# A gated-linear-attention block on one Trainium2 core: part of the operands made ahead is stored unsplit and split after loading

## The chip, the core and the metric

The kernel runs on one core of a Trainium2 chip. The core has five engines with a queue each: TensorE (PE; its weight loads are listed as PEld), VectorE (DVE), ScalarE (ACT), GpSimd (POOL) and SyncE (SP), which in this kernel issues the DMA transfers. Each engine takes its own instructions in order; between engines they wait on semaphores. The metric is the device time of one execution in microseconds, and the time of a kernel is the median of its runs.

## What is computed

One decoder block over 2048 positions of width 1024: a normalised input goes through one combined input projection into two mixers, a gated linear attention with 4 heads and a short gated convolution; their outputs go through an output projection and a residual add, then a feed-forward part with a residual add and a last normalisation.

```python
h = rmsnorm(x, norm1_g[l])
proj = h @ w_in[l]
p_q, p_k, p_v, p_g, p_a, c_b, c_c, c_h = jnp.split(proj, splits, axis=-1)
...
log_a = (jax.nn.log_sigmoid(gate_logits) / GATE_NORMALIZER)...
o = gla_chunked(q, k, v, log_a)
o = rmsnorm(o, gla_norm_g[l]) * jax.nn.silu(p_g)
u = c_c * c_h
o_conv = c_b * causal_depthwise_conv(u, conv_w[l])
mixed = jnp.concatenate([o_gla, o_conv], axis=-1) @ w_out[l]
x = x + mixed
h2 = rmsnorm(x, norm2_g[l])
ffn = (jax.nn.silu(h2 @ w_ffn_gate[l]) * (h2 @ w_ffn_up[l])) @ w_ffn_down[l]
x = x + ffn
```

Everything is float32.

## The kernel before

**Products of halves.** Activations are held transposed, features on the 128 partitions and positions along the free dimension, 512 positions to a tile. The 2048 positions are worked in two halves of 1024 (two tiles of 512, j = 0 and 1). A matrix product of one half with two blocks of 128 columns is a "unit": a two-by-two block product, done as in Strassen-Winograd with seven products instead of eight (`PRODUCTS`, line 35). The weight side of the seven is A11, S1, S2, A12, S3, S4, A22, and the input side is B11, T1, T2, B21, T3, B22, T4. The T's are differences of input blocks, the S's sums and differences of weight blocks that POOL makes (lines 342 to 349).

**Split operands.** A float32 operand is used as a pair: a rounded high part, made by ACT as a copy to `float32r`, and the rest, made by DVE as a subtraction (`split`, line 145, whose two instructions are lines 146 and 147). A product step is three matmuls of 128x128 weights with 128x512 inputs: high by high, high by rest, rest by high (`product_step`, lines 359 to 361). One product of a unit is four such steps over k. So each input operand is a buffer `op` of shape [128, 2, 512], and 28 of them (seven kinds, four k) serve all units of a half. The pool `opp` has just 28 such buffers. A unit's weights are split as it goes (`weight_quarter`, tile `wq`, four buffers).

**The first half** is built from loads (`build_first`). During its twelve input-projection units (`in_proj(0)`), background work is run in small steps, one for every second product (`tick`): the gates, row statistics, then `h1_ahead`, then the recurrence of the first half (`gla_half`).

**The second half's operands** are made ahead by `h1_ahead` (line 509). `combine` (line 222) loads the eight raw tiles of each half column, scales them on DVE (line 483), lets POOL make the differences (lines 247 to 260), and hands each of the 28 results to `put`, for each k in the order B11, T1, T2, T3, B21, T4, B22. `put` splits it into two scratch tiles, `hi` and `lo`, and stores both into DRAM (`s_h1`, seen in the trace as `siB` and `siT`). The scratch tiles come from a pool of 11 (`bx`), shared with everything else that the background does.

When the first half's units are all issued, `load_pairs(s_h1)` (line 519) loads the 28 pairs into `op` buffers, 512 KB each, in the order of `PRODUCTS`: B11, T1, T2, B21, T3, B22, T4. Each load waits until the buffer that it takes has had its last reader in the first half's last unit. All loads and stores go through the queue of SP (lines 138 and 141). Then come the second half's gates and its twelve units (`in_proj(1)`).

**Order.** The program text gives the dependences; the order of instructions on each engine is fixed when the kernel is built, by the tile framework's scheduler, and `issue_after` pins a few by hand. On the chip each engine follows that order.

Of the kernel before, what the change touches and what calls it, by code (L numbers as in the profile page):

```python
# [10 lines left out]
F32 = mybir.dt.float32  # L11
F32R = mybir.dt.float32r
# [6 lines left out]
P = 128  # L19
D = 1024  # L20
SEQ = 2048
PB = 512
# [12 lines left out]
PRODUCTS = [  # L35
    ("A11", "B11"), ("S1", "T1"), ("S2", "T2"), ("A12", "B21"),
    ("S3", "T3"), ("S4", "B22"), ("A22", "T4"),
]


LATER = ("B21", "T3", "B22", "T4")


C_G1, C_G2, C_GF, C_BG, C_GN, C_CW = 0, 8, 16, 24, 26, 27
# [4 lines left out]
def tile_hymba_block(ctx, tc, x, xt, win, wa, wgu, wout, wffn, wdown, wdown_first, small, out):  # L49
# [3 lines left out]
    def pool_of(name, bufs, **kw):  # L53
        return ctx.enter_context(tc.tile_pool(name=name, bufs=bufs, **kw))

    const = pool_of("const", 1)
    opp = pool_of("opp", 28)
# [5 lines left out]
    dram = pool_of("dram", 1, space=DRAM)  # L63
# [34 lines left out]
    def scratch(name, n):  # L98
# [17 lines left out]
    ]  # L116
    s_h2 = {n: [dram.tile([P, PB], F32, name=f"sf{n}_{k}") for k in range(4)] for n in LATER}
    s_h2p = {
        n: [dram.tile([P, 2, PB], F32, name=f"sh{n}_{k}") for k in range(4)] for _, n in PRODUCTS
    }  # L120
    s_h1 = {
        n: [dram.tile([P, 2, PB], F32, name=f"si{n}_{k}") for k in range(4)] for _, n in PRODUCTS
    }

    def col(c):
# [11 lines left out]
    def load(dst, src):  # L137
        return nc.sync.dma_start(dst, src)

    def store(dst, src):  # L140
        return nc.sync.dma_start(dst, src)
# [3 lines left out]
    def split(src, hi, lo):  # L145
        last_hi[:] = [act.activation(hi, src, AF.Copy)]  # L146
        return dve.tensor_tensor(lo, src, hi.bitcast(F32), ALU.subtract)  # L147
# [71 lines left out]
    def no_operands():  # L219
        return {b: [] for _, b in PRODUCTS}  # L220

    def combine(src, g, rb, put):


        order = [kj for k in range(4) for kj in ((k, 0), (k, 1), (k + 4, 1), (k + 4, 0))]
        ahead = deque()

        def fetch():
            if order:
                k, j = order.pop(0)  # L230
                h = bt("h")
                load(h[:], src(k, j))
                ahead.append((k, j, h))

        def quad():
            k, j, h = ahead.popleft()
            fetch()
            return scaled(col(g + k), rb[j], h)

        fetch()  # L240
        fetch()
        for k in range(4):
            b11 = quad()
            put("B11", k, b11)
            yield
            b12, t1 = quad(), bt("t1")
            pool.tensor_tensor(t1[:], b12[:], b11[:], ALU.subtract)
            put("T1", k, t1)
            yield
            b22 = quad()  # L250
            pool.tensor_tensor(t1[:], b22[:], t1[:], ALU.subtract)
            put("T2", k, t1)
            yield
            pool.tensor_tensor(b12[:], b22[:], b12[:], ALU.subtract)
            put("T3", k, b12)
            yield
            b21 = quad()
            put("B21", k, b21)
            yield
            pool.tensor_tensor(t1[:], b21[:], t1[:], ALU.subtract)  # L260
            put("T4", k, t1)
            yield
            put("B22", k, b22)
            yield
# [236 lines left out]
    def build_h():  # L501


        def quad(k, j):
            return scaled(col(C_G1 + k), rbs[j], raws[j, k])

        return build_first(quad, first_weights)

    def h1_ahead():

        def put(n, k, h):
            hi, lo = [bx[0].tile([P, PB], F32R, name=e, tag="b") for e in ("hi", "lo")]
            split(h[:], hi[:], lo[:])
            for e, y in enumerate((hi, lo)):
                store(s_h1[n][k][:, e, :], y[:].bitcast(F32))

        yield from combine(lambda k, j: xt[2 + j, :, k, :], C_G1, (rbs[2], rbs[3]), put)

    def load_pairs(src):
        ops = no_operands()  # L520
        for _, n in PRODUCTS:
            ops[n] = [load_pair(p) for p in src[n]]
        return ops

    def load_pair(src):
        o = opp.tile([P, 2, PB], F32R, name="op", tag="op")
        load(o[:].bitcast(F32), src[:])
        return o
# [279 lines left out]
    def h2_first(ssq, ops):  # L808
# [10 lines left out]
        def put(n, k, h):  # L819
            if n in LATER:  # L820
                store(s_h2[n][k][:], h[:])
            else:
                ops[n].append(split_op(h[:]))
# [3 lines left out]
    def h2_rest(ops):  # L827
        hs = deque()
        order = [(n, k) for n in LATER for k in range(4)]

# [205 lines left out]
    ops, first, differences = build_h()  # L1036
# [7 lines left out]
    in_proj(0, ops, first, differences)  # L1044
    drain_background(lambda: len(background) < 2)
    ops = load_pairs(s_h1)
    background.append(gate(1, ops))
    in_proj(1, ops)
# [120 lines left out]
```

## Time and profile before

| | |
|---|---|
| median of 3 runs | 2122.82 us (2122.73 to 2124.79) |
| profiled execution, its own time | 2120.33 us |
| its span | 2118.6 us |
| mean granted clock of TensorE | 0.989 |
| HBM read and written | 300.63 MB and 168.30 MB |
| stores of `hi` and `lo` by `h1_ahead` | 56 of 256 KB, issued from 140.6 to 229.6 us |
| loads of the 28 pairs | 28 of 512 KB, issued from 275.9 to 314.4 us |
| the second half's gate product (line 541) | up to 474 us |

In the profile, a line of the timeline has the start in us, the duration, the engine, the source line, the operation, the tiles written and read, and how often; in brackets behind it stands the engine's idle time just before and what ended it. An instruction made by a helper carries the helper's line: all splits are lines 146 and 147 and are told apart by their tiles (`hi`, `lo`, `wq`, `op`). "DMA to landing" is the time from the issue of a transfer on SP to its completion. Ends of matmuls are modelled, and their pitch, 0.23 us here, is shorter than their listed duration of 0.39.

### The profile page before, as it was taken

To read this page: it belongs to the slowest core of one execution; us is meant where nothing else is said; L and a number is where in the kernel's file an instruction comes from. 1 tells how busy PE (TensorE), PEld (TensorE's weight loads), DVE (VectorE), ACT (ScalarE), POOL (GpSimd) and SP (SyncE) were. 2 spreads that over 40 slices of the span, in tenths; PEclk is the share of its full clock that TensorE was granted. 3 is DMA by queue.
4 is the path that set the end of the run, shared out by engine and by line. 5 is a ranking of instruction groups with operands and counts; after the bars stand their busy time and mean duration, and the time that the engine had idled before them with its cause. 6 is when DMAs were issued, how large, how long until landed. Compare 5 with 4: busy or idle time off the path is not lost.

```text
span 2118.6 us, 26920 instructions
## 1 busy us (share of the span) xinstructions
PE 2038.3 (96%) x9133; PEld 1651.9 (78%) x9133; DVE 1412.8 (67%) x1983; ACT 1014.8 (48%) x1997; POOL 973.8 (46%) x703
## 2 busy tenths in 40 slices
PE   6999999999999999999999999999999989999996
PEld 4777787887888887778888878787888878877774
DVE  7668775548754696887887565555776766665554
ACT  5555444656543345544545453333554554543344
POOL 3435322222102364555564348764635544436774
PEclk9999999999999999999999999999999999999998
DMA  7349586433586882655655687697455535587662
GB/s 277 125 150 317 184 328 225 137 110 123 181 310 211 335 286 91 232 220 185 232 190 204 229 331 269 236 340 312 150 206 185 200 138 189 181 345 279 268 268 110
DMA packets 190971, 470.74 MB, mean 222 GB/s; under 512 B 20016, under 2 KB 65264, under 8 KB 181232
## 3 DMA queue, kind: packets, MB, share of 16 engines
q1 hardware_dynamic: 190832, 469.01, 60.8%
q8 instruction: 72, 1.18, 0.2%
q14 instruction: 67, 0.55, 0.1%
HBM read 300.63 MB, written 168.30 MB: 221 GB/s over the span
## 4 chain that ended last, share of the span: by engine, by line
PE 78%; DVE 8%; DMA 6%; issue 3%; ACT 2%; POOL 2%; SPq 0%; DVEq 0%; ACTq 0%; POOLq 0%
PE mm L359 22%; PE mm L361 22%; PE mm L360 22%; PE mm L777 2%; PE mm L778 2%; PE mm L780 2%; DVE wq L147 2%; DVE so L147 1%; DMA op<-shT 1%; DMA raw<-in_wffn_dram 1%; DMA raw<-in_wdown_dram 1%; PE a_ps L541 1%; DVE op L147 1%; ACT wq L146 1%; DMA raw<-in_win_dram 1%
## 5 line engine op out<-in xcount | busy, mean ns | idle before, releaser
L359 PE MATMUL mm<-op,wq 128*128 128x512 f32 x2499 | 983.0, 395 | 27.0 <-ACT c L379 10.7
L361 PE MATMUL mm<-op,wq 128*128 128x512 f32 x2499 | 968.3, 393 | 15.2 <-DVE wq L147 14.2
L360 PE MATMUL mm<-op,wq 128*128 128x512 f32 x2499 | 977.6, 391 | 0.0
L147 DVE TENSOR_TENSOR wq<-raw,wq 128x512 fp32r<-128x512 f32 (+2 forms) x626 | 523.3, 843 | 338.6 <-ACT wq L146 336.3
L146 ACT ACTIVATE wq<-raw 128x512 fp32r<-128x512 f32 (+2 forms) x626 | 363.9, 587 | 563.1 <-PE mm L361 407.0
L359 PEld LDWEIGHTS mm<-op,wq 128*128 128x128 f32 x2499 | 471.7, 189 | 141.8 <-ACT c L379 14.8
L361 PEld LDWEIGHTS mm<-op,wq 128*128 128x128 f32 x2499 | 471.5, 189 | 127.9 <-DVE wq L147 29.0
L360 PEld LDWEIGHTS mm<-op,wq 128*128 128x128 f32 x2499 | 472.0, 189 | 97.2 <-issue 1.0
L344 POOL TENSOR_TENSOR raw<-s,raw 128x512 f32<-128x512 f32 (+2 forms) x97 | 128.3, 1323 | 441.7 <-DVE wq L147 421.6
L383 DVE TENSOR_TENSOR c<-mm,c 128x512 f32<-128x512 f32 x267 | 182.9, 685 | 98.4 <-PE mm L361 94.7
L342 POOL TENSOR_TENSOR s<-raw 128x512 f32<-128x512 f32 (+2 forms) x97 | 130.0, 1340 | 206.7 <-DMA raw<-in_wffn_dram 84.8
L349 POOL TENSOR_TENSOR raw<-raw 128x512 f32<-128x512 f32 (+2 forms) x97 | 125.1, 1290 | 139.6 <-DVE wq L147 132.4
L379 ACT ACTIVATE c<-mm 128x512 f32<-128x512 f32 x267 | 154.7, 585 | 39.8 <-PE mm L361 37.4
L759 POOL TENSOR_TENSOR ssx<-ssx,q 128x512 f32<-128x512 f32 x52 | 76.1, 1476 | 155.4 <-ACT q L758 155.2
L343 POOL TENSOR_TENSOR raw<-raw 128x512 f32<-128x512 f32 (+2 forms) x97 | 137.4, 1416 | 4.1
L948 POOL TENSOR_TENSOR y<-c,y 128x512 f32<-128x512 f32 x66 | 98.7, 1498 | 49.0 <-DVE c L383 48.7
L147 DVE TENSOR_TENSOR so<-t,so 128x512 fp32r<-128x512 f32 x100 | 91.0, 916 | 23.6 <-ACT so L146 23.0
L146 ACT ACTIVATE wq<-s 128x512 fp32r<-128x512 f32 (+2 forms) x97 | 56.8, 586 | 95.4 <-PE mm L361 88.6
L777 PE MATMUL mm<-op,wq 128*128 128x512 f32 x256 | 100.9, 395 | 0.0
L778 PE MATMUL mm<-op,wq 128*128 128x512 f32 x256 | 99.8, 390 | 0.0
L147 DVE TENSOR_TENSOR wq<-s,wq 128x512 fp32r<-128x512 f32 (+2 forms) x97 | 85.0, 876 | 15.7 <-ACT wq L146 15.1
L146 ACT ACTIVATE so<-t 128x512 fp32r<-128x512 f32 x100 | 62.3, 626 | 39.2 <-DMA sa_B<-so 14.6
(175 smaller groups left out, 1884.4 us busy)
## 6 DMA issues: line engine op xcount, KB each, us to landing
raw<-in_wffn_dram SPq DMA_DIRECT2D x44, 1024.0 KB, 5.5
sa_T<-so SPq DMA_DIRECT2D x88, 512.0 KB, 5.0
op<-sa_T SPq DMA_DIRECT2D x88, 512.0 KB, 8.7
sa_B<-so SPq DMA_DIRECT2D x69, 512.0 KB, 3.4
op<-sa_B SPq DMA_DIRECT2D x69, 512.0 KB, 9.1
raw<-in_win_dram SPq DMA_DIRECT2D x23, 1024.0 KB, 5.3
raw<-in_wdown_dram SPq DMA_DIRECT2D x24, 768.0 KB, 6.2
sx<-y SPq DMA_DIRECT2D x48, 256.0 KB, 3.2
```

Of the source, the lines that this page charges most:

```text
L146: last_hi[:] = [act.activation(hi, src, AF.Copy)]
L147: return dve.tensor_tensor(lo, src, hi.bitcast(F32), ALU.subtract)
L342: pool.tensor_tensor(s1, a21, a22, ALU.add)
L343: pool.tensor_tensor(a21, a11, a21, ALU.subtract)
L344: pool.tensor_tensor(a11, s1, a11, ALU.subtract)
L359: pe.matmul(o[:], wh, xh, start=first and k == 0, stop=False, skip_group_check=True)
L360: pe.matmul(o[:], wh, xl, start=False, stop=False, skip_group_check=True)
L361: return pe.matmul(o[:], wl, xh, start=False, stop=k == n - 1, skip_group_check=True)
L379: act.activation(t[:], o[:], AF.Copy)
L383: dve.tensor_tensor(t[:], o[:], t[:], ALU.add)
L777: pe.matmul(o[e, j][:], wh, m[:, 0, :], start=k == 0, stop=False)
L778: pe.matmul(o[e, j][:], wh, m[:, 1, :], start=False, stop=False)
```

## The change

The three input kinds used last in a unit, T3, B22 and T4, are handled in another way; the other four (B11, T1, T2, B21) stay as they were.

- Their twelve DRAM tiles have one plane instead of two.
- In `h1_ahead`, `put` stores the unsplit tile and returns: no `hi`, no `lo`, one store of 256 KB.
- `load_whole` takes an `op` buffer, loads the unsplit tile into its second plane (256 KB), and splits it there: ACT writes the rounded part into the first plane, DVE subtracts and writes the rest over the loaded values.

```diff
+WHOLE = ("T3", "B22", "T4")
...
+    def made_ahead(name, n):
+        return dram.tile([P, PB] if n in WHOLE else [P, 2, PB], F32, name=name)
+
     s_h1 = {
-        n: [dram.tile([P, 2, PB], F32, name=f"si{n}_{k}") for k in range(4)] for _, n in PRODUCTS
+        n: [made_ahead(f"si{n}_{k}", n) for k in range(4)] for _, n in PRODUCTS
     }
...
         def put(n, k, h):
+            if n in WHOLE:
+                store(s_h1[n][k][:], h[:])
+                return
             hi, lo = [bx[0].tile([P, PB], F32R, name=e, tag="b") for e in ("hi", "lo")]
             split(h[:], hi[:], lo[:])
...
-            ops[n] = [load_pair(p) for p in src[n]]
+            ops[n] = [(load_whole if n in WHOLE else load_pair)(p) for p in src[n]]
         return ops
+
+    def load_whole(src):
+
+        o = opp.tile([P, 2, PB], F32R, name="op", tag="op")
+        load(o[:, 1, :].bitcast(F32), src[:])
+        split(o[:, 1, :].bitcast(F32), o[:, 0, :], o[:, 1, :])
+        return o
```

## The prediction

> **What bounds the kernel now.** I read the page first, then a table by stretches around the two places that the change touches, then the idle times of PE there.
>
> ```profile
> span 2118.6 us, 26920 instructions
> PE 2038.3 (96%) x9133; PEld 1651.9 (78%) x9133; DVE 1412.8 (67%) x1983; ACT 1014.8 (48%) x1997; POOL 973.8 (46%) x703
> PE 78%; DVE 8%; DMA 6%; issue 3%; ACT 2%; POOL 2%; SPq 0%; DVEq 0%; ACTq 0%; POOLq 0%
> ```
>
> PE is busy 96% of the span and holds 78% of the chain that ended last. So a few vector operations more or less count only where PE stands idle for them. The whole idle time of PE is 2118.6 - 2038.3 = 80 us, and only the part near the change can be won.
>
> The table by stretches has, behind the stretch and its length, busy us (instructions) of PE, PEld, DVE, ACT and POOL, then the granted clock, the DMA share and GB/s.
>
> ```profile
> 140.00:230.00 90.00, 82.71 (x349) 65.72 (x348) 81.89 (x103) 51.57 (x95) 51.00 (x32) 0.98 0.79 276
> 230.00:276.00 46.00, 43.71 (x184) 34.99 (x183) 31.07 (x45) 17.78 (x36) 15.28 (x10) 0.96 0.50 159
> 276.00:300.00 24.00, 24.00 (x115) 19.62 (x114) 18.53 (x27) 10.78 (x22) 5.90 (x5) 1.00 0.97 374
> 300.00:315.00 15.00, 15.00 (x83) 11.86 (x82) 9.10 (x19) 8.67 (x25) 2.92 (x3) 1.00 1.03 410
> 315.00:340.00 25.00, 23.31 (x115) 18.88 (x113) 12.96 (x23) 10.51 (x28) 6.76 (x5) 1.00 0.81 283
> ```
>
> From 140 to 230 us the second half's operands are made ahead, between the matmuls of the first half. There DVE is busy 91% and PE loses 7.3 us; PE loses 2.3 us more up to 276. From 276 to 315 the 28 operand pairs are loaded: the DMA engines are full (374 to 410 GB/s), PE has no idle time at all, and DVE has 11.4 us free of 39, ACT 19.6. So the two ends of the change lie in opposite stretches: it takes work from one where DVE decides and puts it into one where PE decides.
>
> PE's own idle times between 140 and 250 us, with their releasers, from the order of time:
>
> ```profile
> 150.49 0.50 PE L361 MATMUL mm<-op,wq 128*128 128x512 f32 x1 [2.08 <-DVE wq L147]
> ...
> 180.75 0.50 PE L359 MATMUL mm<-op,wq 128*128 128x512 f32 x1 [1.59 <-ACT c L379]
> ...
> 204.16 0.50 PE L361 MATMUL mm<-op,wq 128*128 128x512 f32 x1 [0.90 <-DVE wq L147]
> ...
> 220.00 0.50 PE L361 MATMUL mm<-op,wq 128*128 128x512 f32 x1 [1.75 <-DVE wq L147]
> ...
> 222.90 0.50 PE L359 MATMUL mm<-op,wq 128*128 128x512 f32 x1 [0.30 <-ACT c L379]
> ...
> 226.99 0.50 PE L361 MATMUL mm<-op,wq 128*128 128x512 f32 x1 [0.61 <-DVE wq L147]
> ...
> 246.09 0.50 PE L359 MATMUL mm<-op,wq 128*128 128x512 f32 x1 [2.08 <-ACT c L379]
> ```
>
> Every one waits for DVE's half of a weight split or for ACT's copy out of a bank: both stand in the same queues as the operand splits. After the first and the last the clock falls:
>
> ```profile
> 150.00:160.00 10.00, 9.51 (x35) 7.66 (x36) 10.00 (x11) 8.55 (x15) 7.31 (x5) 0.83 0.55 203
> 240.00:250.00 10.00, 7.81 (x28) 5.67 (x28) 7.94 (x13) 4.70 (x10) 1.85 (x2) 0.87 0.69 211
> ```
>
> A granted clock of 0.87 over 10 us costs at most 1.3 us more behind the stall at 246.
>
> **What is removed.** Of 28 splits made ahead, 12 go (T3, B22 and T4, four each): 12 ACT copies and 12 DVE subtractions. Of 56 stores of 256 KB, 12 go, and 24 of the scratch buffers are no longer taken. Their kinds in the trace (min/median/max ns):
>
> ```profile
> L146 ACT ACTIVATE hi<-h x16: 613/626/640, 140.0 to 226.5; 128x512 fp32r<-128x512 f32 x16
> L147 DVE TENSOR_TENSOR lo<-h,hi x16: 679/686/1781, 145.7 to 228.7; 128x512 fp32r<-128x512 f32 x16
> L147 DVE TENSOR_TENSOR c<-c,hi x16: 677/682/1779, 233.1 to 601.3; 128x512 fp32r<-128x512 f32 x16
> L147 DVE TENSOR_TENSOR lo<-t,hi x12: 676/688/1393, 151.0 to 226.9; 128x512 fp32r<-128x512 f32 x12
> ```
>
> The order per k is B11, T1, T2, T3, B21, T4, B22; counted off along DVE's subtractions, the removed ones of the last two k that stand in DVE's long backlog are these (single ones, with their neighbours):
>
> ```profile
> 204.02 0.68 DVE L147 TENSOR_TENSOR lo<-t,hi 128x512 fp32r<-128x512 f32 x1
> 204.62 0.68 DVE L147 TENSOR_TENSOR wq<-raw,wq 128x512 fp32r<-128x512 f32 x1
> 205.22 0.69 DVE L147 TENSOR_TENSOR lo<-h,hi 128x512 fp32r<-128x512 f32 x1
> ...
> 220.47 1.78 DVE L147 TENSOR_TENSOR lo<-h,hi 128x512 fp32r<-128x512 f32 x1
> ...
> 226.86 0.68 DVE L147 TENSOR_TENSOR lo<-t,hi 128x512 fp32r<-128x512 f32 x1
> ...
> 228.72 0.68 DVE L147 TENSOR_TENSOR lo<-h,hi 128x512 fp32r<-128x512 f32 x1
> ...
> 248.76 0.42 DVE L666 TENSOR_TENSOR kq<-kq,ee 128x256 f32<-128x256 f32 x1 [1.87 <-ACT ee L664]
> ```
>
> DVE stands in one unbroken queue from about 203 us to the idle time that ends at 248.76. In such a queue an instruction costs its pitch: 0.68 long, 0.60 from one start to the next (204.02, 204.62, 205.22), so 0.08 less than its length. The five removed ones cost 0.60 x 4 + 1.70 = 4.1 us. The idle times of PE in that stretch are 0.90 + 1.75 + 0.30 + 0.61 + 2.08 = 5.6 us, so 4.1 fits under them; of the clock's 1.3 us I take 1.0, as the idle time at 246, the last in the queue, should shrink most. **Gain here 5.1 us**, bounds 2 (the backlog is filled by waits for loads instead) and 5.6 + 1.3 = 6.9.
>
> The other seven removed subtractions lie between 158 and 200 us, where one idle time of PE stands, at 180.75. The ACT instruction ahead of that bank copy had waited for a scratch buffer:
>
> ```profile
> 178.58 0.63 ACT L146 ACTIVATE hi<-h 128x512 fp32r<-128x512 f32 x1 [1.51 <-DMA siT<-hi]
> ```
>
> With two buffers less per removed kind that wait should go: **gain 1.0 us** of 1.59, bounds 0 and 1.6. The stall at 150.49 lies ahead of the first removed split and stays.
>
> The 1.78 us of one subtraction against a median of 0.686 is a row to dwell on: it is in a stretch where POOL is busy 51 of 90 us. The Trainium skill (SBUF — State Buffer, Who interferes with whom) says that a DVE instruction with two SBUF inputs and a GpSimd instruction that reads SBUF hold one read interface in turn, the second waiting until the first is through. By that rule, the trace agrees, and each split moved to 276 to 315 us, where POOL is busy 8.8 us of 39, is cheaper there than it was.
>
> **What is added.** 12 ACT copies and 12 DVE subtractions behind the loads of T3, B22 and T4, and loads of 256 KB in place of 512 KB. Writing in place has its price in the trace: c<-c,hi takes 682 ns, as much as into another buffer (686). At the pitch that is 12 x 0.60 = 7.2 us of DVE and less of ACT, against 11.4 and 19.6 us free before 315 us. PE covers it: it runs without idle time through this stretch, and ACT and DVE wait for it there:
>
> ```profile
> 303.76 1.15 ACT L146 ACTIVATE wq<-raw 128x512 fp32r<-128x512 f32 x2 [4.20 <-PE mm L361]
> ...
> 322.50 0.63 ACT L146 ACTIVATE wq<-raw 128x512 fp32r<-128x512 f32 x1 [5.34 <-PE mm L361]
> ```
>
> So the operations cost nothing as long as they don't wait; without that cover, 7.2 us.
>
> The new wait is the danger. A split stands in the in-order queues of ACT and DVE until its load has landed, and behind it stand the weight splits (L146, L147), the bank copies (L379, L408) and sums (L383), and the recurrence's copies. SP issues the loads as the last unit of the first half frees their buffers, and they land late (issue, then the median from issue to landing of T3, B22, T4):
>
> ```profile
> 292.67 1.61 SPq L138 DMA_DIRECT2D op<-siT  x2
> ...
> 301.70 4.13 SPq L138 DMA_DIRECT2D op<-siB  x4
> ...
> 310.58 4.13 SPq L138 DMA_DIRECT2D op<-siT  x4
> ```
>
> ```profile
> op<-siT SPq DMA_DIRECT2D x4, 512.0 KB, 11.2
> ...
> op<-siB SPq DMA_DIRECT2D x4, 512.0 KB, 8.8
> ...
> op<-siT SPq DMA_DIRECT2D x4, 512.0 KB, 7.6
> ```
>
> T3's first load lands about 304 us, whatever its own size, since the backlog ahead of it is full pairs. If the queue reaches its copy near 296, ACT is held up to 8 us. PE has then the weights of two or three products in hand, 12 matmuls of 0.227 us each (2.7 us a product), so about 5.5 us are hidden. The three kinds move 12 x 262 KB = 3.1 MB less, which at 410 GB/s drains the queue up to 7.7 us sooner, so B22 and T4 land earlier than now. I take **1.1 us** for all three waits, near the one such row there is (a split behind a load, before the feed-forward part), because it issues to landing 7 to 8 us as well:
>
> ```profile
> 786.79 0.63 ACT L146 ACTIVATE op<-h 128x512 fp32r<-128x512 f32 x1 [1.83 <-DMA h<-sfB]
> ```
>
> Bounds 0 and, for three batches, 8.6: the first held 8 + 4 x 0.60 - 5.5 = 4.9, the next two, with landings of about 5 us out of a drained queue, 5 + 2.4 - 5.5 = 1.9 each.
>
> Of the size there is a rule that speaks against the change: the Trainium skill (DMA: Bandwidth & Descriptors, Anatomy of one DMA) gives a fixed 2.0 us per transfer beside bytes / 436 GB/s. By that, as an estimate, a halved load takes 2.6 us instead of 3.2, so almost nothing lands sooner; the trace's 7.6 to 11.2 us are queueing, which the rule leaves out, and there bytes count.
>
> **The sum.** -5.1 - 1.0 + 1.1 = -5.0 us. The profiled execution took 2120.3 us (span 2118.6 and 1.7 around it), so it would be 2115.3; the median of the runs is 2122.8, 2.5 above it, so 2117.8.
>
> **The rivals.**
> (a) The gain goes further: with fewer scratch buffers and 12 stores less also the waits for loads in 160 to 200 us go, and the whole upper bounds come: -6.9 - 1.6 = -8.5, 2114.3. For it: all those idle times hang on one queue. Against: the first backlog's stall at 150 remains.
> (b) Nothing is won: PE's idle times move to the next wait, for raw weights or for POOL's differences of weights, since the order on each engine is fixed at build time and a faster DVE waits for the same partners: 2122.8 within 2. For it: POOL at 51 of 90 us; against: no idle time of PE in the stretch names POOL or a DMA.
> (c) The other side, slower: the splits are queued on ACT and DVE near their loads' issue, and hold the weight splits and bank copies behind them. At 8.6 us of stalls plus three falls of the clock at 1.3 us each the cost is 12.5, against a gain of 6.1: +6.4, 2129.2. It decides from 6.1 us of stalls on. For it: landings of 7.6 to 11.2 us; against: ACT's weight splits there wait 4.20 and 5.34 us for PE before they start, so a hold of that length ahead of them delays nothing, and the weights are two products ahead.
> (d) The change does something else than it says: the halves are shared by one buffer, so a pair is complete only when the subtraction has overwritten its source; should matmuls be tied to whole buffers, only the 12 matmul groups wait 0.6 us more, which is inside (c)'s cost.
>
> **How the numbers follow.** Less than 0.2%, 4.2 us, can't be told from no change here. Forecast 0.50 (2113 to 2121 as its own range; 0.40 of it beyond 4.2 us), (a) 0.10, (b) 0.10, (c) with (d) 0.30, of which 0.28 beyond 4.2. Faster 0.40 + 0.10 = 0.50; within 0.10 + 0.10 + 0.02 = 0.22; slower 0.28. The range from 2111 to 2131 holds the forecast, most of (a), (b) and (c) up to 2131, and leaves out some 0.15.
>
> **What would show it.** Right: DVE's busy time from 140 to 230 us lower by 8 to 10 us with no unbroken queue up to 248; idle times of PE at 204 to 246 gone or halved, the granted clock of that stretch at 1.00; only 16 pairs of hi and lo; 12 splits whose ACT copies wait under 2 us for their loads; PE without idle time from 276 to 330. Wrong: ACT or DVE held for over 5 us by loads of T3, PE idle behind weight splits near 300 to 330, or the same sum of idle times of PE in 140 to 250 behind other releasers.

## The result, and the profile after

| | before | changed |
|---|---|---|
| median | 2123.11 us (6 runs) | 2111.14 us (6 runs) |
| ratio to before, 95% interval | | 0.9948 [0.9935, 0.9962] |
| the same kernels once more, in a later set | 2123.47 us (29 runs) | 2111.94 us (6 runs), 0.9945 [0.9926, 0.9964] |
| profiled execution: its time, span | 2120.33, 2118.6 us | 2110.86, 2109.1 us |

The kernel became faster by 11 to 12 us; 5.0 were forecast, 8.5 in rival (a). The 2111.1 us lie below the forecast's own 2113 to 2121 and below rival (a)'s 2114.3.

The page of the changed kernel begins:

```profile
span 2109.1 us, 26874 instructions
PE 2033.1 (96%) x9133; PEld 1648.9 (78%) x9133; DVE 1418.4 (67%) x1983; ACT 1014.1 (48%) x1997; POOL 972.4 (46%) x703
```

The counts are those of before, since splits were moved and none was dropped. No engine's work fell; what fell is time in which PE stood still or ran at a lower clock. The changed kernel by stretches (length, busy us and instructions of PE, PEld, DVE, ACT, POOL; granted clock, DMA share, GB/s):

```profile
140.00:230.00 90.00, 86.97 (x378) 70.22 (x377) 86.90 (x108) 49.24 (x91) 52.91 (x34) 1.00 0.83 280
230.00:264.00 34.00, 34.00 (x152) 28.10 (x151) 18.84 (x26) 13.94 (x27) 11.03 (x8) 1.00 0.30 111
264.00:290.00 26.00, 26.00 (x124) 21.26 (x123) 20.50 (x30) 11.46 (x23) 7.82 (x5) 1.00 0.91 356
290.00:305.00 15.00, 15.00 (x81) 11.76 (x80) 11.43 (x22) 11.61 (x30) 2.53 (x2) 1.00 1.05 396
305.00:330.00 25.00, 25.00 (x136) 20.45 (x135) 21.69 (x37) 14.52 (x39) 7.34 (x5) 1.00 0.55 170
```

DVE is busier from 140 to 230 us than before (86.9 against 81.9), though twelve subtractions left: work that came later before is now inside the window. A fixed window compares two kernels badly when one runs ahead; the same piece of work has to be found in both. All idle times of PE between the start-up and 625 us, from the order of time of the changed kernel, without the start-up's other ones:

```profile
65.16 0.79 PE L368 MATMUL mm<-op,wq 128*128 128x512 f32 x1 [2.06 <-DVE wq L154]
...
151.46 0.50 PE L368 MATMUL mm<-op,wq 128*128 128x512 f32 x1 [2.11 <-DVE wq L154]
...
160.60 0.50 PE L366 MATMUL mm<-op,wq 128*128 128x512 f32 x1 [0.86 <-ACT c L386]
...
408.89 0.50 PE L366 MATMUL mm<-op,wq 128*128 128x512 f32 x1 [0.61 <-DVE c L390]
...
617.00 0.63 PE L703 MATMUL v_ps<-ident,vt 128*128 128x128 f32 x4 [0.91 <-ACT carry L710]
```

Two of them, at 65 and 409 us, stand in every kernel here and are used as marks. The same marks before, with an idle time between them that the changed kernel has not:

```profile
64.49 0.80 PE L361 MATMUL mm<-op,wq 128*128 128x512 f32 x1 [2.06 <-DVE wq L147]
...
331.72 0.50 PE L359 MATMUL mm<-op,wq 128*128 128x512 f32 x1 [1.69 <-ACT c L379]
...
420.78 0.50 PE L359 MATMUL mm<-op,wq 128*128 128x512 f32 x1 [0.62 <-DVE c L383]
```

A third mark lies between: the first load of an operand of the second half, which waits for PE's last unit of the first half. Its row gives first and last start (before, then changed):

```profile
L138 SPq DMA_DIRECT2D op<-siB x12: 319/320/383, 275.9 to 305.5; - x12
```

```profile
L145 SPq DMA_DIRECT2D op<-siB x12: 319/320/382, 265.4 to 294.1; - x12
```

So the way from the start-up mark to the loads shrank from 275.9 - 64.49 = 211.4 to 265.4 - 65.16 = 200.2 us, and the way from the loads to the last mark from 144.9 to 143.5 us. Behind the last mark the changed kernel took 1700.2 us to its end against 1697.8; the idle time at 617, which before did not have, is part of that. What else adds to it isn't shown.

PE's seven idle times between 140 and 250 us were 9.31 us; two are left, 2.97 us. The two clock falls of before are not in this profile either (1.00 throughout). By the rows that the prediction quotes they cost 1.7 and 1.3 us; the second went on past its row (0.92 granted from 250 to 255 us), so it is 1.7 too. A stall also lengthens the gap between two matmul starts by 0.17 us beyond its idle time and the pitch (148.01 to 150.49: 2.48 against 2.08 + 0.23), 0.9 us for five stalls. Idle time, falls and gaps, 6.3 + 3.4 + 0.9, make 10.6 of the 11.2 us.

DVE's unbroken queue now begins and ends here (order of time of DVE, changed kernel):

```profile
177.51 1.47 DVE L154 TENSOR_TENSOR lo<-h,hi 128x512 fp32r<-128x512 f32 x1 [0.83 <-ACT hi L153]
...
230.79 2.71 DVE L154 TENSOR_TENSOR c<-c,hi 128x512 fp32r<-128x512 f32 x2 [0.70 <-ACT hi L153]
```

It runs dry some 17 us sooner than before (at 230.1 against 246.9), and PE no longer waits inside it. Five waits for loads of raw tiles, 4.6 us in all, which DVE had from 167 to 202 us before, are gone too. The two longest (order of time of DVE, before):

```profile
169.53 0.75 DVE L483 SCALAR_TENSOR_TENSOR h<-h,sml,rb_ps 128x512 f32<-128x512 f32 x1 [1.84 <-DMA h<-in_xt_dram]
...
176.56 0.75 DVE L483 SCALAR_TENSOR_TENSOR h<-h,sml,rb_ps 128x512 f32<-128x512 f32 x1 [1.43 <-DMA h<-in_xt_dram]
```

Of ACT's waits for a scratch buffer that a store still holds, four before and 7.4 us in all, one is left, and it is longer than any of the four (order of time of ACT, changed kernel):

```profile
176.84 0.63 ACT L153 ACTIVATE hi<-h 128x512 fp32r<-128x512 f32 x1 [3.46 <-DMA siT<-hi]
```

The late splits, and the whole list of waits of all splits into `op` that names a DMA:

```profile
L153 ACT ACTIVATE op<-op x12: 615/624/636, 295.6 to 308.2; 128x512 fp32r<-128x512 f32 x12
...
  DMA h<-sfB: 1.6, 1
```

```profile
L154 DVE TENSOR_TENSOR op<-op x12: 677/684/1456, 296.3 to 312.8; 128x512 fp32r<-128x512 f32 x12
```

The one wait for a DMA belongs to another stage (`sfB`, before the feed-forward part). No late split waited for its load. The transfers, issue to landing, of T3 (two and two), B22 and T4:

```profile
op<-siT SPq DMA_DIRECT2D x2, 256.0 KB, 11.9
...
op<-siT SPq DMA_DIRECT2D x2, 256.0 KB, 8.7
...
op<-siB SPq DMA_DIRECT2D x4, 256.0 KB, 5.2
...
op<-siT SPq DMA_DIRECT2D x4, 256.0 KB, 5.3
```

T3's first loads, behind a backlog of full pairs, took as long as before (11.2); B22 and T4 landed 2 to 4 us sooner than before (8.8 and 7.6).

### The profile page after: what moved, and what is told of

Its sections match the earlier page's. It is cut to its first block, busy times and chain, and to the rows that moved or that the text cites. A ratio compares the mean times of both kernels' runs of the same rounds, so it can differ in the third digit from the quotient of the medians.

```text
span 2109.1 us, 26874 instructions
## 1 busy us (share of the span) xinstructions
PE 2033.1 (96%) x9133; PEld 1648.9 (78%) x9133; DVE 1418.4 (67%) x1983; ACT 1014.1 (48%) x1997; POOL 972.4 (46%) x703
## 4 chain that ended last, share of the span: by engine, by line
PE 70%; DVE 8%; DMA 7%; ACT 3%; issue 3%; POOL 2%; SPq 0%; DVEq 0%; ACTq 0%; POOLq 0%
PE mm L366 21%; PE mm L368 21%; PE mm L367 21%; DVE wq L154 2%; DMA op<-shT 1%; DVE so L154 1%; PE mm L794 1%; DVE h L490 1%; PE mm L795 1%; PE mm L797 1%; DVE op L154 1%; DMA sx<-y 1%; ACT wq L153 1%; PE o_ps L718 1%; DMA shT<-so 1%
## 5 line engine op out<-in xcount | busy, mean ns | idle before, releaser
L366 PEld LDWEIGHTS mm<-op,wq 128*128 128x128 f32 x2499 | 470.8, 188 | 137.6 <-ACT wq L153 12.3
```

The lines of the kernel that those rows point to most:

```text
L366: pe.matmul(o[:], wh, xh, start=first and k == 0, stop=False, skip_group_check=True)
```

## The experiments

All are built on the changed kernel, unless said. Times are medians, ratios are to the kernel before, run beside them, with 95% intervals. "To the loads" and "from the loads" are the two ways between the marks in the profiled execution, and "rest" is its time from the last mark to its end.

| kernel | median us | ratio | to the loads | from the loads | rest |
|---|---|---|---|---|---|
| before, first and second profile | 2123.1 | 1 | 211.4, 211.2 | 144.9, 144.9 | 1697.8, 1698.9 |
| changed, first and second profile | 2111.1, 2111.9 | 0.9948, 0.9945 | 200.2, 197.5 | 143.5, 143.4 | 1700.2, 1700.0 |
| e1: early splits made again | 2120.9 | 0.9982 [0.9972, 0.9992] | 210.4 | 143.5 | 1699.7 |
| e7: early DVE part alone made again | 2123.2 | 0.9995 [0.9983, 1.0007] | 211.2 | 143.5 | 1703.7 |
| e6, e6b: stores of before | 2117.0, 2117.1 | 0.9967 [0.9954, 0.9979], 0.9968 [0.9955, 0.9980] | 201.7, 202.5 | 143.5, 143.4 | 1703.2, 1703.5 |
| e5: load bytes of before | 2117.8 | 0.9976 [0.9963, 0.9989] | 199.0 | 150.1 | 1703.8 |
| e2: both | 2120.7 | 0.9985 [0.9976, 0.9994] | 203.2 | 149.7 | 1701.8 |
| e3: no late splits | 2111.0 | 0.9939 [0.9925, 0.9953] | 199.2 | 144.8 | 1699.4 |
| e4: a weight split held | 2121.3 | 0.9990 [0.9977, 1.0004] | 198.8 | 150.9 | 1699.2 |
| w2: two kinds | 2118.1 | 0.9976 [0.9964, 0.9988] | 203.7 | 145.4 | 1703.3 |
| w4: four kinds | 2117.9 | 0.9975 [0.9963, 0.9986] | 199.7 | 145.7 | 1705.5 |

One profile's way to the loads is good to some 1.5 us (200.2 and 197.5 are one kernel; their mean is 198.9, that of before 211.3). The rest spreads over 8 us from kernel to kernel, in stages that no edit here touches, though two profiles of one kernel agree within 1.1. What makes it differ isn't shown, so the ways between the marks carry the argument, not the medians alone.

**Is it the vector work, or the stores?** e1 puts the twelve early splits back, into tiles that nobody reads:

```diff
             if n in WHOLE:
+                hi, lo = [bx[0].tile([P, PB], F32R, name=e, tag="b") for e in ("hi", "lo")]
+                split(h[:], hi[:], lo[:])
                 store(s_h1[n][k][:], h[:])
                 return
```

> The changed kernel (2111.1 us), with the twelve early splits of T3, B22 and T4 made again into scratch tiles that nobody reads; the unsplit tiles are stored and split late as in the change. So the vector work and the scratch buffers of before come back, the stores do not. Theory A (the gain is DVE and ACT time in the crowded stretch): PE's idle times between 200 and 250 us come back, 2119 to 2124. Theory B (the gain is the twelve stores less and their bytes): 2111 to 2113.

2120.9 us, and the way to the loads is 210.4: the whole early gain is gone. The order of time of PE in e1 has these idle times where the changed kernel has one, of 0.86:

```profile
160.23 0.80 PE L366 MATMUL mm<-op,wq 128*128 128x512 f32 x1 [2.20 <-ACT c L386]
...
182.69 0.50 PE L366 MATMUL mm<-op,wq 128*128 128x512 f32 x1 [1.60 <-ACT c L386]
...
215.76 0.50 PE L368 MATMUL mm<-op,wq 128*128 128x512 f32 x1 [1.57 <-DVE wq L154]
...
226.45 0.50 PE L366 MATMUL mm<-op,wq 128*128 128x512 f32 x1 [1.67 <-ACT c L386]
```

e7 puts back DVE's part alone, in the same places: no ACT copy, one scratch tile.

```diff
             if n in WHOLE:
+                lo = bx[0].tile([P, PB], F32R, name="lo", tag="b")
+                dve.tensor_tensor(lo[:], h[:], h[:], ALU.subtract)
                 store(s_h1[n][k][:], h[:])
```

> The changed kernel with twelve DVE subtractions (of a tile from itself, into scratch tiles that nobody reads) put back where the early ones stood, without the ACT copies and with half of the scratch buffers. If DVE's time alone makes the gain: as e1, 203 us or more from the start-up stall to the first load (200 in the changed kernel, 210 in e1), 2117 to 2122. If ACT's copies or the buffers make it: 200 to 202 us, 2111 to 2114.

2123.2 us and 211.2 us to the loads, as much as before: twelve DVE subtractions with one scratch tile each are worth the whole way's 12 us, and neither ACT's copies nor the second scratch tile adds to it. The releasers in e7:

```profile
161.71 0.50 PE L366 MATMUL mm<-op,wq 128*128 128x512 f32 x1 [1.89 <-ACT c L386]
...
184.49 0.79 PE L366 MATMUL mm<-op,wq 128*128 128x512 f32 x1 [3.41 <-ACT c L386]
...
218.05 0.50 PE L368 MATMUL mm<-op,wq 128*128 128x512 f32 x1 [1.56 <-DVE wq L154]
```

Here the releaser misleads: where PE waited for ACT's bank copy, ACT itself had stood, just ahead of that copy, and by the profile it stood for a scratch buffer that one of the added subtractions (`lo`, line 521) had still to write (order of time of ACT, e7):

```profile
159.53 0.63 ACT L153 ACTIVATE hi<-h 128x512 fp32r<-128x512 f32 x1 [2.99 <-DVE lo L521]
...
182.32 0.63 ACT L153 ACTIVATE hi<-h 128x512 fp32r<-128x512 f32 x1 [6.29 <-DVE lo L521]
```

Leaving ACT's copies out doesn't remove these stalls; leaving DVE's subtractions out does. But part of their price comes by way of the pool of 11 scratch buffers, which they hold while they stand in DVE's queue. No run puts DVE's time back without a scratch tile, or a scratch tile without DVE's time, so the two aren't separated.

**The bytes.** e2 stores the unsplit tile into both planes and loads both, and splits late:

```diff
-                store(s_h1[n][k][:], h[:])
+                for e in range(2):
+                    store(s_h1[n][k][:, e, :], h[:])
...
-        load(o[:, 1, :].bitcast(F32), src[:])
+        load(o[:].bitcast(F32), src[:])
```

> The changed kernel with all bytes of before: the unsplit tile is stored twice, into both planes, and both planes are loaded (512 KB) before the split in place. So 56 stores and full loads as before, the splits late. Theory A: 2111 to 2114, PE idle no more than in the changed kernel. Theory B: 2119 to 2124, with waits for stores and loads.

2120.7 us: the number of theory B, but the trace does not say B. The way to the loads is 203.2 us, 8.1 us shorter than before's 211.3, so two thirds of the early gain are still there. The loss is behind the loads (order of time of PE, e2):

```profile
323.15 0.50 PE L367 MATMUL mm<-op,wq 128*128 128x512 f32 x1 [0.79 <-DVE op L154]
...
325.65 0.50 PE L367 MATMUL mm<-op,wq 128*128 128x512 f32 x1 [1.54 <-DVE op L154]
```

PE waits for the late splits themselves (`op`). So e5 and e6 separate loads and stores. e5 loads the unsplit tile into both planes, 512 KB by two loads, and stores it once:

```diff
-        load(o[:, 1, :].bitcast(F32), src[:])
+        for e in range(2):
+            load(o[:, e, :].bitcast(F32), src[:])
```

> The changed kernel with the load bytes of before alone: the unsplit tile is loaded into both planes (two loads of 256 KB), then split in place; the stores stay at 44. Theory C (the late splits are hidden only because the halved loads land before the queues of ACT and DVE reach them): the stretch before the loads as in the changed kernel, PE idle behind a late split near 320 us, 2115 to 2120. If the second e2 loss came from the stores' bytes: 2111 to 2113 and no such wait.

2117.8 us: nothing lost ahead of the loads, 6.6 us behind them (150.1 against 143.5). In e5 (order of time of PE, and the row of the stretch around it):

```profile
321.18 0.51 PE L367 MATMUL mm<-op,wq 128*128 128x512 f32 x1 [1.74 <-DVE op L154]
...
323.62 0.80 PE L366 MATMUL mm<-op,wq 128*128 128x512 f32 x1 [1.69 <-ACT c L386]
```

```profile
320.00:330.00 10.00, 7.13 (x20) 5.37 (x21) 5.23 (x8) 3.85 (x8) 3.52 (x3) 0.66 0.70 212
```

With full loads the last late split starts on DVE at 320.4 us instead of 312.8, PE waits for it, and the clock falls to 0.66 over these 10 us. The late splits are hidden with halved loads and not with full ones, but not in the way of theory C: no late split of e5 waits for a load. The last one follows other work without idle time on both engines (order of time of ACT, then of DVE, e5):

```profile
317.22 1.14 ACT L153 ACTIVATE wq<-raw 128x512 fp32r<-128x512 f32 x2
318.26 0.62 ACT L153 ACTIVATE op<-op 128x512 fp32r<-128x512 f32 x1
```

```profile
320.44 0.68 DVE L154 TENSOR_TENSOR op<-op 128x512 fp32r<-128x512 f32 x1
```

The 256 KB loads take 5.3 us in the median from issue to landing in e5 too, but T4's are issued from 302.1 us instead of 297.3, and the late splits stand later in the order of ACT and DVE, among the recurrence's work. That order is fixed when the kernel is built; how the size of the loads comes to change it isn't shown.

e6 keeps the 256 KB loads and stores twice, as in e2.

> The changed kernel with the stores of before alone: the unsplit tile is stored twice, the loads stay at 256 KB. By e2's first stretch the stores cost some 3 us ahead of the loads (203.2 against 200.2 us from the start-up stall to the first load) and nothing after: 2112 to 2116. Theory B (all of e2's loss is the stores): 2119 to 2122.

2117.0 us, over its range by 1, though the way to the loads grew by only 1.5 us against the changed kernel's first profile. It was run again in one set with the changed kernel:

> The kernel of e6 again, beside the changed kernel: the stores stored twice. In e6's profile the stretch up to 411 us was only 1.5 us longer than the changed kernel's, the median 6 us. If the 6 us are real: 1.002 to 1.004 of the changed kernel; if they lie in the sets: within 0.1 percent of 1.0007.

0.9968 against 0.9945 in one set, 1.0023 of the changed kernel. These two intervals overlap, but over both sets the 24 runs of this kernel have a median of 2117.1 us, the changed kernel's twelve 2111.1, so the loss is real. By the means of two profiles each, the way to the loads is 202.1 - 198.9 = 3.2 us longer (1.5 and 5.0 in the single pairs); its DMA share from 140 to 230 us is 0.83 in the changed kernel. Another 3 us are added behind the last mark (1703.2 and 1703.5 against 1700.2 and 1700.0), where this edit changes nothing; what makes them isn't shown.

> The changed kernel once more, beside the others of this set: 2110 to 2112, ratio 0.994 to 0.996. If it comes out near 2116, the sets differ by more than the kernels in them.

The changed kernel came out at 2111.9, so the sets don't differ by more than this.

**What the late splits cost.** e3 has none; it leaves out the split of T3, B22 and T4 in the second half and loads the unsplit tile into both planes:

```diff
-        load(o[:, 1, :].bitcast(F32), src[:])
-        split(o[:, 1, :].bitcast(F32), o[:, 0, :], o[:, 1, :])
+        for e in range(2):
+            load(o[:, e, :].bitcast(F32), src[:])
```

> The changed kernel without the twelve late splits: the unsplit tile is loaded into both planes by two loads of 256 KB. It leaves out the split of T3, B22 and T4 in the second half, so these operands count twice and what follows from them differs. If the late splits are hidden under PE: 2110 to 2112. If they cost what they take (7.2 us of DVE): 2104 to 2106.

2111.0 us: on balance they cost nothing that can be measured. e3 loads the full 512 KB, as e5 does, so against e5 it prices the late splits behind full loads: 5.3 us on the way from the loads. e3 even has an idle time back that before had at 331.72 us and the changed kernel has not (order of time of PE, e3):

```profile
320.31 0.50 PE L366 MATMUL mm<-op,wq 128*128 128x512 f32 x1 [1.69 <-ACT c L386]
```

So the 1.4 us won behind the loads go with that idle time. Whether the late splits or the halved loads took it away isn't shown, since e3 has neither.

**What a held weight split costs.** The rival (c) of the prediction was a weight split that stands behind a late split. e4 makes it so, for S2 in the second half's first unit:

```diff
+        held.append(last_hi[0])
...
-        w["S2"] = weight_quarter(a11)
+        with ExitStack() as stack:
+            if held:
+                stack.enter_context(tc.issue_after(held[3].ins))
+                held.clear()
+            w["S2"] = weight_quarter(a11)
```

> The changed kernel with one order pinned: in the second half's first unit the weight split of S2 (and what follows it on ACT) may only stand behind the fourth late split of T3. It prices the rival of the prediction, a weight split held by a load. T3's fourth load lands about 297 us, S2's split goes from 285 to about 300 us, and its product is due near 298: PE idle 2 to 6 us near 300 to 305 and the clock falls once, 2113 to 2119. If ACT's order there has slack: 2111.

2121.3 us, over its range. Order of time of PE, then of ACT, in e4:

```profile
299.36 0.79 PE L370 MATMUL mm<-op,wq 128*128 128x512 f32 x1 [6.10 <-ACT wq L153]
```

```profile
298.16 0.63 ACT L153 ACTIVATE op<-op 128x512 fp32r<-128x512 f32 x1
298.68 1.66 ACT L153 ACTIVATE wq<-raw 128x512 fp32r<-128x512 f32 x3
```

The weight split came at 298.7 us instead of 285.4; PE ran out of weights and stood still for 6.1 us. The way behind the loads is 7.4 us longer. The mechanism of (c) is real: against the changed kernel in the same set (2111.9) it takes 9.4 of the 11.5 us won; the order of the changed kernel keeps clear of it, since its late splits stand at 295.6 us and later, behind the weight splits.

**How many kinds.** w2 has `WHOLE = ("B22", "T4")`, w4 has `("B21", "T3", "B22", "T4")`.

> Two kinds (B22, T4) stored whole in place of three. If each moved split takes its pitch out of DVE's queue: two thirds of the gain, 2114 to 2117. If the gain has a threshold (DVE's queue must run dry before the recurrence starts): 2118 or more.

> Four kinds (B21 too). In the changed kernel only 0.86 us of idle time of PE is left behind the first removed split, so at most 1 to 2 us more are to be won before the loads, and DVE, at 95 to 99 percent from 300 to 320 us, gets four more splits, which are needed earlier: 2110 to 2116; over 2116 if these splits hold PE as in e2.

w2, 2118.1 us: with eight splits moved, these idle times are left in the early stretch (order of time of PE, w2):

```profile
179.28 0.50 PE L366 MATMUL mm<-op,wq 128*128 128x512 f32 x1 [1.85 <-ACT c L386]
...
211.16 0.50 PE L368 MATMUL mm<-op,wq 128*128 128x512 f32 x1 [1.21 <-DVE wq L154]
```

By its median w2 falls to the expectation's threshold (2118 or more), but the way to the loads doesn't show one. It is 203.7 us: eight moved splits win 7.6 us, the third kind's four another 4.8, against the mean of the changed kernel's two profiles, 198.9. w2's profile has 2 us more than the changed kernel's on the way from the loads, too, and 3 more behind the last mark. w4, 2117.9 us, over its range: the way to the loads is that of three kinds (199.7), so B21 wins nothing more there, and behind the loads PE waits for the recurrence's small DVE operations, which stand among 16 late splits (order of time of PE, w4):

```profile
309.47 0.47 PE L366 MATMUL mm<-op,wq 128*128 128x512 f32 x1 [2.34 <-DVE hsq L165]
```

The way from the loads is 2.2 us longer with it; another 5 us are added behind the last mark and stay unexplained. Three kinds are the best of those tried, and no version here that computes the same beat the change.

**The clock.** The kernel before, profiled once more:

> The kernel before, once more, for a second profile of it. If the clock's two falls (after the idle times that end at 150 and 246 us) belong to those idle times, they are there again, with 0.8 to 0.9 granted over 10 us each. If they are chance, at least one is missing and its loss of 1.3 to 1.7 us with it, at a time within 2121 to 2125.

The stretch around the first idle time and the one around the last, before again:

```profile
145.00:160.00 15.00, 12.92 (x50) 10.12 (x50) 14.90 (x17) 10.96 (x19) 9.36 (x7) 0.89 0.68 239
...
245.00:265.00 20.00, 18.17 (x80) 15.06 (x81) 9.20 (x15) 7.61 (x15) 5.44 (x4) 1.00 0.48 143
```

The fall after 150 us is there again, the one after 246 is not, behind the same idle time of 2.09 us; another one stands at 180 to 190 us. So it is chance whether one idle time brings a fall. The idle time at 150 us, 2.08 to 2.11 us long, is in all 14 profiles: the clock fell after it in 9 and did not in 5, the changed kernel's first profile among the 5 and its second among the 9.

## Why the prediction was right, and where its sizes were off

Right in sign, and right that the gain is vector work taken out of the early stretch and hidden later; the size was less than half of what was measured, and the reason given for one term did not hold.

- **The gain is DVE's work in the early stretch.** Right, and shown by e7, which puts back the subtractions with one scratch tile each and loses all of it; DVE's time and the scratch tile are not separated. PE's idle times at 180 to 246 us went, as the prediction expected of those from 204 on.
- **Gain in DVE's backlog, 5.1 us, and for the seven other splits, 1.0 us: mis-sized.** The whole early way shrank by 11.2 us in the first pair of profiles and by 13.7 in the second. The step that failed is the cut of the stretch at 203 us: only the five subtractions behind it were priced in full, because DVE has some idle time from 160 to 200 us. All twelve belong to the price. By their starts in the profile before, eight have a pitch of 0.60 or 0.61, three of 1.05 to 1.70, and one is listed with its neighbour (2.49 for both, half taken): 9.9 us in all. e7 says 211.2 against 198.9: 12.3. What lies above 9.9 would be restarts and clock falls; that division of it is worked out, not tried. w2 gives one check: the four splits of T3 have 5.1 us of pitch, and with them left early the way is 4.8 us longer.
- **The reason given for the 1.0 us did not hold.** The stall of PE at 180.75 was put down to ACT's wait of 1.51 us for a scratch buffer, three instructions ahead of the bank copy. In the changed kernel ACT waits 3.46 us for one, three instructions ahead of a bank copy again (at 178.38), and PE does not stall behind it. The stall went, but such a wait alone does not make it.
- **The bounds, 6.9 and 1.6 us, were too tight.** They were sums of PE's idle times with one clock fall; the measured gain went past both together by 2.7 us. The stall at 150 us does remain, as said, but the clock's fall behind it need not.
- **The stores were priced at nothing by themselves.** They and their bytes are worth 3.2 us on the way to the loads (e6). The two prices are not additive. Against before's 211.3 us, e6, which has these stores without the vector work, is 9.2 us shorter to the loads; e1, which has the vector work without these stores, 0.9; the changed kernel, which has neither, 12.4.
- **Rival (a), 8.5 us, came nearest, and was passed.** The waits for loads that it names went: DVE had five before, 4.6 us in all, and has none in the changed kernel. But e1 and e7 have none either, and have lost the gain, so these waits are not what it is made of.
- **The late splits, 1.1 us: right to be small, measured at nothing** (e3). The cover named is the one that hides them. Each was cheaper late, as said: four of the twelve subtractions took 1.1 us or more before, one does now. The three waits for landings, 8.7 us at most by the prediction's terms (it writes 8.6), did not come at all. B22 and T4 landed sooner, as said. With the bytes back (e5) the same splits cost 6.6 us, though by a later place in the order and not by a wait for a landing. The Trainium skill (DMA: Bandwidth & Descriptors, Anatomy of one DMA) gives its rule there for transfers issued from GpSimd, while all here go through SP; by it, as an estimate, a load of half the size lands only 0.6 us sooner. Measured in this full queue are 2 to 4 us, and the measurement decides.
- **Rival (c), slower by 6.4: did not come.** Its mechanism is real: one held weight split costs 7.4 us on the way behind the loads (e4), against 4.9 and a clock fall of 1.3 put on the first batch, and a late split that comes too late 6.6 (e5).
- **DVE's busy time from 140 to 230 us lower by 8 to 10 us: wrong.** It rose by 5.0, as later work moved into the window. The sign to look for was the end of the unbroken queue, 246.9 against 230.1 us.

## What to carry to other kernels

In a stretch where one in-order engine is the limit, price every instruction that leaves it, not only those in its unbroken queue, and add what each stall costs beyond its idle time (here a longer gap and, by chance, a clock fall). Work that must be done either way is best put where its engine has room, but the place has to be checked on two counts: that the data is there before the queue reaches it, and that what stands behind it (weight splits, bank copies) has lead time. When deferring a conversion also halves the transfer, as here, price the saved bytes too: without them 6.6 us behind the loads were lost. And compare a variant stage by stage: here up to 5 us lay in stages that the edit doesn't touch.

## What was not expected of the hardware

The granted clock fell after idle times of PE as short as 2.1 us, and not every time: after the idle time at 150 us in 9 of 14 profiles. Such a fall, to 0.89 over 15 us, costs 1.7 us, nearly as much as the idle time itself. The Trainium skill (TensorE: Matmul & The Clock Gate, What's actually happening) gives an idle window of about 3.4 us before the clock falls; the runs here show falls after 2.1. And twelve stores of 256 KB, put into a stretch with a DMA share of 0.83, cost some 3 us there, though no idle time of PE names a DMA.
